# Order of the gate matrices, of the first value block and of the gate loads in a PEER layer

## The chip, the cores and the metric

The kernel runs on one NeuronCore of a Trainium2 chip. The metric is the device time of one execution in microseconds (us), lower is better; the time of a kernel is the median of its runs. Engines are named as the profile names them: PE (TensorE matmul), PEld (its weight loads), DVE (VectorE), ACT (ScalarE), POOL (GpSimd) and SP (SyncE, which only issues transfers here).

## The reference

One decoder layer for 512 tokens of width 1024. An attention sub-layer comes first (two groups of heads, not touched here). The second sub-layer is a mixture of 16384 one-neuron experts: each token looks up its 16 best experts for each of 8 heads with product keys, and sums their outputs.

```python
sc = jnp.einsum("bshpd,hpnd->bshpn", qp, sub_keys)      # two halves, 128 keys each
s1, i1 = lax.top_k(sc[..., 0, :], 16); s2, i2 = lax.top_k(sc[..., 1, :], 16)
cand = s1[..., :, None] + s2[..., None, :]
top_s, top_c = lax.top_k(cand.reshape(..., 256), 16)
expert = e1 * 128 + e2                                  # e1, e2 from i1, i2, top_c
gate = jax.nn.softmax(top_s, axis=-1)
a = einsum("bcd,bchkd->bchk", h, peer_u[expert])        # u_e . h
y = einsum("bchk,bchkd->bcd", gate * gelu(a), peer_v[expert])
x = x + gate2 * y
```

## The kernel before

The 512 tokens are four tiles of 128. Tile 0 (`SPARSE`) is done by gathers: 128 rows of `peer_u` and 128 of `peer_v` are fetched per token by indirect transfers from POOL, and DVE forms the dot products (`scr`, `sact`) and the weighted sum (`y`). Tiles 1 to 3 (`DENSE`, 384 tokens) are done densely against all 16384 experts, in 128 blocks of 128 experts, in two long loops.

The **unit blocks** (`ahead`, then `dense_u`): block b of U (`ut`, 512 KB) is loaded, split into a rounded part `uhi` (ACT) and a rest `ulo` (DVE), and multiplied with the hidden states in 24 matmuls of 384 columns (L935 to L937). ACT applies gelu (`ge`, L939), and for the first 120 blocks (`AHEAD`) the 192 KB result is stored to DRAM (`ged`).

The **value blocks** (`dense`): `ge` of block b comes back (L947), DVE multiplies it with the gates of that block (`gt`, L968), ACT and DVE split the product into `whl` (L971, L972), the block of V (`vt`, 512 KB) is split into `vhi` (ACT, L871) and `vlo` (DVE, L872), and 18 matmuls of 512 columns add it to six accumulators in PSUM (`acc`, L981). The last eight unit blocks are computed between value blocks.

The gates are dense matrices `G`, made from the lookup. For each dense tile `pick(i)` (12 steps, `choose` and `select`, on DVE and POOL) finds the 16 experts of each head, and `gates(i)` (48 steps in all, `gate_matrix`) builds 0/1 patterns on DVE, multiplies them on PE (16 short matmuls a step, L820), copies them out on ACT (`gst`, L822) and writes 1 MB to `G` every second step (L826). `work` is the list of these steps; the loop at the end of `build` takes some of them after each unit block.

`gt` holds the gates of eight value blocks (`GI`), 1536 KB, in two buffers. Buffers that the prediction uses: `whl` comes from pool `k3` with six buffers (L85), so its copy for block n waits until PE has finished block n - 6; `uhi`, `ulo`, `vhi` and `vlo` have two each (L870), so the copy to `vhi` for block m waits until PE has finished block m - 2; `ut` and `vt` have three.

The order of the instructions on each engine is not the order of the source. The pools and data set what may run, and a scheduler with its own estimate of times (`schedule_with_timeline_sim`) fixes one order for each engine when the kernel is built. Each engine then works strictly in that order.

Of the kernel before, what the change touches and what calls it, by code (L numbers as in the profile page):

```python
# [21 lines left out]
P = 128  # L22
# [9 lines left out]
NK = 128  # L32
# [6 lines left out]
DENSE = [1, 2, 3]  # L39
ND_T = len(DENSE) * P  # L40
GT = 16
NG = ND_T // GT
GI = 8
GSCALE = 4096.0
OT = 8
AHEAD = 120
# [32 lines left out]
class Layer:  # L79
# [814 lines left out]
    def ahead(self):  # L894

        self.ge = {}
        self.acc, self.vs = None, {}
        self.reopen()
        for b in range(AHEAD):
            self.dense_u(b)  # L900
            yield

    def dense(self):

        u = AHEAD
        for b in range(3):
            self.ge_in(b)
        for b in range(NK):
            self.ge_in(b + 3)
            self.v_in(b)  # L910
            if b < NK - 2:
                for t in range(len(DENSE)):
                    self.v_mm(b, t)
            elif b == NK - 1:
                for t in range(len(DENSE)):
                    self.v_mm(b - 1, t)
                    self.v_mm(b, t)
                    self.finish(DENSE[t], self.acc[t])
            for _ in range(min(NK - u, self.u_count(b, u))):
                self.dense_u(u)  # L920
                u += 1
            yield
# [4 lines left out]
    def dense_u(self, b):  # L927
        nc = self.nc
        pe = nc.tensor
        uh, ul = self.us.pop(b) if b in self.us else self.u_load(b)  # L930
        pa = self.bank() if b < AHEAD else self.bank2()
        A = pa[:, :ND_T]
        for k in range(KD):
            hh, hl = (z[k // 2][:, k % 2, :] for z in self.h2)
            pe.matmul(A, uh[:, k, :], hh, start=(k == 0), stop=False)  # L935
            pe.matmul(A, uh[:, k, :], hl, start=False, stop=False)  # L936
            pe.matmul(A, ul[:, k, :], hh, start=False, stop=(k == KD - 1))  # L937
        self.ge[b] = self.k2([P, ND_T], "ge")
        nc.scalar.activation(self.ge[b], A, AF.Gelu_apprx_tanh)  # L939
        if b < AHEAD:  # L940
            nc.sync.dma_start(self.ged[b], self.ge.pop(b))
# [4 lines left out]
            self.ge[b] = self.k2([P, ND_T], "ge")  # L946
            self.load(self.ge[b], self.ged[b])  # L947

    def gates_in(self, n):

        self.gtn = self.dn([P, NG, GI, GT], "gt")
        self.load(self.gtn, self.G[n])

    def v_in(self, b):

        nc, I = self.nc, self.I
        if b == 0:
            self.gates_in(0)
        if b % GI == 0:
            self.gt = self.gtn  # L960
        if b % GI == 4 and b + 4 < NK:
            self.gates_in(b // GI + 1)
        vt = self.dn([P, D], "vt", F32, 3)
        self.load(vt, I["peer_v"][b * P:(b + 1) * P, :])
        vh, vl = self.split(vt, "v", nc.vector)
        w = self.ge.pop(b)
        wg = w.rearrange("p (g t) -> p g t", t=GT)
        nc.vector.tensor_tensor(out=wg, in0=wg, in1=self.gt[:, :, b % GI, :], op=OP.mult)  # L968
        whl = self.k3([P, 2, ND_T], "whl", F32R)
        wh, wl = whl[:, 0], whl[:, 1]  # L970
        nc.scalar.copy(wh, w)  # L971
        nc.vector.tensor_tensor(out=wl, in0=w, in1=wh, op=OP.subtract)  # L972
        if self.acc is None:
            self.acc = [[self.bank(name="acc") for _ in range(2)] for _ in DENSE]
        self.vs[b] = (wh, vh), (wh, vl), (wl, vh)
# [24 lines left out]
    def build(self):  # L1000
# [17 lines left out]
        def seq(*gs):  # L1018
            for g in gs:
                yield from g  # L1020

        def weave(main, fill, n, skip=0, every=1, rest=True):
            for m, _ in enumerate(main):
                if m >= skip and (m - skip) % every == 0:
                    for _ in range(n):
                        next(fill, None)
            if rest:
                run(fill)
# [6 lines left out]
        def top(i, c):  # L1035
            self.best(i, T[i], c)
            yield
# [9 lines left out]
        def pick(i):  # L1047
            for hh in range(2):
                yield from self.choose(i, T[i], hh)

        def gates(i):
            yield from self.gate_matrix(i, *self.chosen[i])
# [32 lines left out]
        n = [self.hidden2(i, T[i]) for i in (3, 2, 1)]  # L1085
        run(pipe(o[:3] + [prep(self.w_pq, 0)] + o[3:5] + n[:1] + o[5:] + [prep(self.w_pq1, 3)] + n[1:] + [q1(3)], 2))
        for c in range(4):
            tops = [top(i, c - 1) for i in DENSE if 0 < c < 3] + ([top(0, 3)] if c == 1 else [])
            weave(self.queries(T, c), seq(*tops), 1)
        work = seq(pick(0), *(top(i, c) for c in (2, 3) for i in DENSE), *(pick(i) for i in DENSE),  # L1090
                   *(gates(i) for i in DENSE))
        sparse = self.sparse_steps(SPARSE)
        share = lambda n, of, steps: (n + 1) * steps // of - n * steps // of if 0 <= n < of else 0

        def gathered(steps):

            for _ in range(steps):
                with self.tc.issue_after(self.last_split.ins):
                    next(sparse, None)

        for n, _ in enumerate(self.ahead()):
            for _ in range(share(n, AHEAD - 8, 102)):
                next(work, None)
            gathered(share(n - 16, AHEAD - 16, 100))
        run(work)
# [50 lines left out]
```

## Time and profile before

| | before |
|---|---|
| median of 3 runs | 1693.03 us (1692.58 to 1693.55) |
| the profiled execution | 1691.5 us, span 1689.1 us |
| mean granted TensorE clock | 0.979 |
| PE busy | 1586.1 us, 94% of the span |
| unit blocks | about 492 to 1086 us |
| value blocks | about 1095 to 1674 us |

The span goes from the first to the last instruction; the execution's time is 2.4 us longer. Durations of matmuls overlap, so the step from one start to the next is what a matmul costs. A figure in brackets at the end of a timeline row is the idle time of that engine ahead of the instruction and what ended it.

### The profile page before, as it was taken

The numbers are of one execution on the slowest core, as the hardware profiler recorded it, in microseconds if no ns is written. First come the engines' busy times: TensorE is split into PE (matmuls) and PEld (weight loads), VectorE is DVE, ScalarE is ACT, GpSimd is POOL, SyncE is SP. The second block draws the span as 40 slices with busy tenths as digits, with TensorE's granted clock in tenths as the row PEclk, the third lists the DMA queues.
The fourth block names the chain that finished last, engine by engine and source line by source line (L and its number), as shares of the span: only waits on it lengthen the run. The fifth ranks groups of instructions, "written<-read, shape, count | busy, mean of one in ns | idle before, by whom it ended". The sixth has DMA issues, their size and how long they took to land.

```text
span 1689.1 us, 25030 instructions
## 1 busy us (share of the span) xinstructions
PE 1586.1 (94%) x8993; PEld 1390.9 (82%) x8993; DVE 1263.2 (75%) x2626; ACT 678.6 (40%) x1072; POOL 478.6 (28%) x514
## 2 busy tenths in 40 slices
PE   5999999998978999999999999799999999999996
PEld 2976498987977999999999999787777777877885
DVE  2624364585899679899989899488888888887863
ACT  3522364354224434334656656333333333333331
POOL 1303510001013355564213232123333333233311
PEclk8999999999989999999999999999999999999998
DMA  7354513368154688888999999999999999999852
GB/s 295 122 212 159 194 39 132 121 215 272 36 188 139 229 287 264 262 281 270 346 335 337 328 325 349 387 354 368 353 370 357 366 365 358 366 375 364 289 180 100
DMA packets 189391, 451.34 MB, mean 267 GB/s; under 512 B 16594, under 2 KB 102610, under 8 KB 185172
## 3 DMA queue, kind: packets, MB, share of 16 engines
q1 hardware_dynamic: 91732, 277.17, 46.1%
q0 software_dynamic: 38656, 139.48, 23.5%
q10 hardware_dynamic: 58880, 33.11, 6.5%
q8 instruction: 70, 1.15, 0.3%
q14 instruction: 53, 0.43, 0.1%
HBM read 393.07 MB, written 56.63 MB: 266 GB/s over the span
## 4 chain that ended last, share of the span: by engine, by line
PE 75%; DVE 11%; DMA 7%; ACT 2%; issue 2%; POOL 0%; POOLq 0%; SPq 0%; DVEq 0%; ACTq 0%
PE acc L981 27%; PE bank L937 8%; PE bank L936 8%; PE bank L935 8%; PE bank L386 4%; PE bank L173 4%; PE bank L387 4%; PE bank L385 4%; DVE ulo L872 3%; PE bank L820 3%; DMA vt<-in_peer_v 2%; PE bank L136 2%; PE bank L564 2%; PE bank L579 2%; DMA ge<-ged 1%
## 5 line engine op out<-in xcount | busy, mean ns | idle before, releaser
L981 PE MATMUL acc<-vhi,whl 128*128 128x512 f32 x1536 | 422.6, 395 | 25.7 <-ACT vhi L871 17.0
L981 PEld LDWEIGHTS acc<-vhi,whl 128*128 128x128 f32 x1536 | 289.0, 189 | 94.1 <-ACT vhi L871 21.7
L937 PE MATMUL bank<-hhi,ulo 128*128 128x384 f32 x1024 | 348.0, 340 | 17.2 <-DVE ulo L872 17.2
L935 PE MATMUL bank<-hhi,uhi 128*128 128x384 f32 x1024 | 346.3, 339 | 12.3 <-ACT uhi L871 12.2
L936 PE MATMUL bank<-hlo,uhi 128*128 128x384 f32 x1024 | 348.3, 340 | 0.0
L831 POOL DMA_INDIRECT gat<-in_peer_v,ids x128 | 158.4, 1238 | 348.2 <-DVE y L859 324.2
L871 ACT CAST uhi<-ut 128x1024 fp32r<-128x1024 f32 x128 | 134.5, 1051 | 304.5 <-PE bank L936 262.4
L981 PE MATMUL acc<-vlo,whl 128*128 128x512 f32 x768 | 241.0, 395 | 0.1
L831 POOL DMA_INDIRECT gat<-in_peer_u,ids x128 | 142.6, 1114 | 336.0 <-DVE sact L849 305.1
L872 DVE TENSOR_TENSOR ulo<-ut,uhi 128x1024 fp32r<-128x1024 f32 x128 | 178.5, 1395 | 63.6 <-ACT uhi L871 62.8
L937 PEld LDWEIGHTS bank<-hhi,ulo 128*128 128x128 f32 x1024 | 194.3, 190 | 23.0 <-DVE ulo L872 22.6
L935 PEld LDWEIGHTS bank<-hhi,uhi 128*128 128x128 f32 x1024 | 194.3, 190 | 14.2 <-ACT uhi L871 13.8
L936 PEld LDWEIGHTS bank<-hlo,uhi 128*128 128x128 f32 x1024 | 194.5, 190 | 0.5
L872 DVE TENSOR_TENSOR vlo<-vt,vhi 128x1024 fp32r<-128x1024 f32 x128 | 156.4, 1222 | 43.6 <-ACT vhi L871 42.7
L871 ACT CAST vhi<-vt 128x1024 fp32r<-128x1024 f32 x128 | 133.7, 1049 | 110.6 <-PE acc L981 85.4
L981 PEld LDWEIGHTS acc<-vlo,whl 128*128 128x128 f32 x768 | 145.1, 189 | 33.1 <-DVE vlo L872 1.2
L859 DVE SCALAR_TENSOR_TENSOR y<-gat,swgt,y 128x1024 f32<-128x1024 f32 x127 | 167.8, 1322 | 1.8 <-DMA gat<-in_peer_v,ids 1.7
L971 ACT CAST whl<-ge 128x384 fp32r<-128x384 f32 x128 | 65.4, 512 | 257.4 <-PE acc L981 240.1
L849 DVE CUSTOM_DVE_ANT_0 scr<-gat,h2r 128x1024 bf16<-128x1024 f32 x128 | 166.2, 1298 | 0.1
L972 DVE TENSOR_TENSOR whl<-ge,whl 128x384 fp32r<-128x384 f32 x128 | 70.8, 555 | 55.6 <-ACT whl L971 52.4
L822 ACT ACTIVATE gst<-bank 128x512 f32<-128x512 f32 x96 | 96.8, 1117 | 9.3 <-PE bank L820 4.7
L968 DVE TENSOR_TENSOR ge<-ge,gt 128x384 f32<-128x384 f32 x128 | 69.8, 552 | 17.7 <-DMA ge<-ged 15.6
(252 smaller groups left out, 2217.2 us busy)
## 6 DMA issues: line engine op xcount, KB each, us to landing
ut<-in_peer_uT SPq DMA_DIRECT2D x128, 512.0 KB
vt<-in_peer_v SPq DMA_DIRECT2D x128, 512.0 KB
G<-gst ACTq DMA_DIRECT2D x24, 1024.0 KB
gt<-G SPq DMA_DIRECT2D x16, 1536.0 KB
ged<-ge SPq DMA_DIRECT2D x120, 192.0 KB
ge<-ged SPq DMA_DIRECT2D x120, 192.0 KB
w<-in_w_ada SPq DMA_DIRECT2D x16, 1024.0 KB
w<-in_w_pq SPq DMA_DIRECT2D x32, 512.0 KB
```

Source lines behind the costliest of these rows:

```text
L822: nc.scalar.activation(st[:, :, q + t4:q + t4 + 4].rearrange("p i t -> p t i"), pb.rearrange("p (t i) -> p t i", t=4), AF.Copy, scale=1.0 ...
L831: self.nc.gpsimd.indirect_dma_start(out=t, out_offset=None, in_=self.I[table], in_offset=bass.IndirectOffsetOnAxis(ap=ids[:, k:k + 1], axi ...
L849: v.tensor_tensor_reduce(out=scr, in0=u, in1=self.rows, op0=OP.mult, op1=OP.add, scale=1.0, scalar=0.0, accum_out=a[:, k:k + 1])
L859: v.scalar_tensor_tensor(out=self.y, in0=t, scalar=w[:, k:k + 1], in1=self.y, op0=OP.mult, op1=OP.add)
L871: nc.scalar.copy(hi, src)
L872: self.last_split = eng.tensor_tensor(out=lo, in0=src, in1=hi, op=OP.subtract)
L935: pe.matmul(A, uh[:, k, :], hh, start=(k == 0), stop=False)
L936: pe.matmul(A, uh[:, k, :], hl, start=False, stop=False)
L937: pe.matmul(A, ul[:, k, :], hh, start=False, stop=(k == KD - 1))
L968: nc.vector.tensor_tensor(out=wg, in0=wg, in1=self.gt[:, :, b % GI, :], op=OP.mult)
L972: nc.vector.tensor_tensor(out=wl, in0=w, in1=wh, op=OP.subtract)
L981: self.nc.tensor.matmul(self.acc[t][half], w[:, ts], v[:, half * 512:(half + 1) * 512], start=(b == n == 0), stop=(b == NK - 1 and n == 2))
```

## The change

The list `work` is reordered: before, all three `pick` and then all three `gates`; now `gates(i)` follows `pick(i)` for each tile. The steps are spread over 108 unit blocks (106 of them) in place of 112 (102). The gates of value block group n are loaded in six parts of 256 KB, called for in six successive value blocks, in place of one load of 1536 KB. Those of the first group, the first three `ge` and the first block of V are called for among the last unit blocks; since this takes the accumulators' six PSUM banks, the last four unit blocks use the other two.

```diff
         for b in range(AHEAD):
             self.dense_u(b)
+            if AHEAD - 5 <= b < AHEAD - 2:
+                for q in range(2):
+                    self.gates_in(0, 2 * (b - AHEAD + 5) + q)
+                self.ge_in(b - AHEAD + 5)
             yield
+            if b == AHEAD - 2:
+                self.v_in(0)
...
     def dense(self):
         u = AHEAD
-        for b in range(3):
-            self.ge_in(b)
         for b in range(NK):
             self.ge_in(b + 3)
-            self.v_in(b)
+            if b:
+                self.v_in(b)
...
-        pa = self.bank() if b < AHEAD else self.bank2()
+        pa = self.bank() if b < AHEAD - 4 else self.bank2()
...
-    def gates_in(self, n):
+    def gates_in(self, n, q):
-        self.gtn = self.dn([P, NG, GI, GT], "gt")
-        self.load(self.gtn, self.G[n])
+        if q == 0:
+            self.gtn = self.dn([P, NG, GI, GT], "gt")
+        g = slice(q * NG // 6, (q + 1) * NG // 6)
+        self.load(self.gtn[:, g], self.G[n, :, g])
...
-        if b == 0:
-            self.gates_in(0)
         if b % GI == 0:
             self.gt = self.gtn
-        if b % GI == 4 and b + 4 < NK:
-            self.gates_in(b // GI + 1)
+        if b % GI < 6 and b // GI + 1 < NK // GI:
+            self.gates_in(b // GI + 1, b % GI)
...
-        work = seq(pick(0), *(top(i, c) for c in (2, 3) for i in DENSE), *(pick(i) for i in DENSE),
-                   *(gates(i) for i in DENSE))
+        work = seq(pick(0), *(top(i, c) for c in (2, 3) for i in DENSE),
+                   *(g for i in DENSE for g in (pick(i), gates(i))))
...
-            for _ in range(share(n, AHEAD - 8, 102)):
+            for _ in range(share(n, AHEAD - 12, 106)):
```

Since the scheduler sets the final order, three places of it are shown, before and after. A row is an instruction with its line, and xN says that it follows itself N times; the changed kernel's lines are five higher from `dense_u` on.

**First place: ACT, from the last unit blocks to the first value blocks.** Before, the copies to `uhi` of blocks 121 to 123 (the row with x3) stand ahead of the first `whl`:

```order
L871 CAST uhi<-ut 128x1024
L939 ACTIVATE ge<-bank 128x384
L871 CAST uhi<-ut 128x1024
L939 ACTIVATE ge<-bank 128x384 x2
L871 CAST uhi<-ut 128x1024 x3
L971 CAST whl<-ge 128x384 x5
L871 CAST vhi<-vt 128x1024
```

Now the first `whl` stands ahead of the copy for block 120 and of the last two gelus:

```order
L871 CAST uhi<-ut 128x1024 x2
L944 ACTIVATE ge<-bank_10965 128x384
L976 CAST whl<-ge 128x384
L871 CAST uhi<-ut 128x1024
L944 ACTIVATE ge<-bank_11006 128x384
L976 CAST whl<-ge 128x384 x2
L871 CAST uhi<-ut 128x1024
L944 ACTIVATE ge<-bank_11061 128x384
L871 CAST vhi<-vt 128x1024 x3
L976 CAST whl<-ge 128x384 x4
L871 CAST uhi<-ut 128x1024
```

The copies for blocks 122 and 123, which PE first needs after value block 109, have moved behind the first value blocks; on PE, value block 0 now starts inside unit block 119, and blocks 120 and 121 lie between value blocks 1 and 5.

**Second place: ACT, at value blocks 26 to 29.** The steady pattern is one `whl` (block n), then one `vhi` (block n - 4). Before, the three `whl` here are those of blocks 30 to 32, and the `vhi` around them those of blocks 25 and 26 and of 27 to 29:

```order
L971 CAST whl<-ge 128x384
L871 CAST vhi<-vt 128x1024 x2
L971 CAST whl<-ge 128x384 x3
L871 CAST vhi<-vt 128x1024 x3
L971 CAST whl<-ge 128x384 x2
L871 CAST vhi<-vt 128x1024
```

Now the `whl` of block 32 stands ahead of the `vhi` of block 27, and that of block 33 ahead of the `vhi` of block 28:

```order
L976 CAST whl<-ge 128x384
L871 CAST vhi<-vt 128x1024
L976 CAST whl<-ge 128x384 x2
L871 CAST vhi<-vt 128x1024
L976 CAST whl<-ge 128x384
L871 CAST vhi<-vt 128x1024 x2
L976 CAST whl<-ge 128x384
```

A `whl` five blocks ahead of the `vhi` that follows it stands in 11 places of the order before and in 14 of the changed one: ahead of the `vhi` of blocks 18, 27, 35, 42, 51, 59, 67, 74, 91, 99 and 106 before, and of 13, 19, 27, 28, 34, 42, 43, 51, 59, 66, 75, 91, 99 and 107 now.

**Third place: the SP queue, at the load of one group's gates.** Before:

```order
L281 DMA vt<-in_peer_v 128x1024
L281 DMA gt<-G 128x3072
L281 DMA ge<-ged 128x384
L281 DMA vt<-in_peer_v 128x1024
L281 DMA ge<-ged 128x384
L281 DMA vt<-in_peer_v 128x1024
```

The same load now; all six parts stand within two value blocks, as at the other groups:

```order
L281 DMA vt<-in_peer_v 128x1024
L281 DMA gt<-G 128x512
L281 DMA ge<-ged 128x384
L281 DMA gt<-G 128x512 x3
L281 DMA vt<-in_peer_v 128x1024
L281 DMA gt<-G 128x512 x2
L281 DMA ge<-ged 128x384
L281 DMA vt<-in_peer_v 128x1024
```

The parts for groups 0 and 1 stand far earlier, in six pairs among the loads of U. The first pair, here, comes after the store of unit block 43, while `gates(1)` is being written:

```order
L946 DMA ged<-ge 128x384
L281 DMA gt<-G 128x512
L281 DMA ut<-in_peer_uT 128x1024
L281 DMA gt<-G 128x512
L946 DMA ged<-ge 128x384
L281 DMA ut<-in_peer_uT 128x1024
```

Before, both groups were loaded one after the other just behind the load of unit block 122.

## Rows read from the trace of the kernel before

**Rows 1.** Page, part 1: busy time of each engine, share, instructions.

```profile
PE 1586.1 (94%) x8993; PEld 1390.9 (82%) x8993; DVE 1263.2 (75%) x2626; ACT 678.6 (40%) x1072; POOL 478.6 (28%) x514
```

**Rows 2.** Busy time by stretch of the span, with granted clock and transfers.

```profile
core 0: us, PE busy (x) PEld busy (x) DVE busy (x) ACT busy (x) POOL busy (x), PEclk, DMA share, GB/s
...
620.00:796.00 176.00, 165.88 (x934) 162.10 (x934) 166.13 (x233) 62.15 (x88) 103.66 (x99) 0.98 0.84 265
796.00:1064.00 268.00, 268.00 (x2029) 259.89 (x2028) 239.00 (x324) 168.47 (x205) 65.22 (x53) 1.00 1.00 338
...
1095.00:1101.00 6.00, 5.86 (x14) 4.60 (x15) 5.20 (x11) 2.10 (x5) 0.00 (x0) 0.50 1.02 366
...
1112.00:1172.00 60.00, 60.00 (x261) 48.66 (x261) 51.85 (x74) 20.06 (x29) 22.81 (x19) 1.00 1.00 388
1172.00:1557.00 385.00, 368.45 (x1589) 297.61 (x1587) 320.20 (x435) 130.99 (x181) 127.43 (x111) 1.00 0.98 365
```

**Rows 3.** Timeline of ACT between unit and value blocks.

```profile
1081.77 1.05 ACT L871 CAST uhi<-ut 128x1024 fp32r<-128x1024 f32 x1 [0.71 <-DMA ut<-in_peer_uT]
1093.49 1.04 ACT L871 CAST uhi<-ut 128x1024 fp32r<-128x1024 f32 x1 [10.67 <-DMA ut<-in_peer_uT]
1094.58 0.51 ACT L971 CAST whl<-ge 128x384 fp32r<-128x384 f32 x1
```

**Rows 4.** Timeline of SP's transfers there.

```profile
1071.95 1.94 SPq L281 DMA_DIRECT2D gt<-G  x2
...
1077.80 0.33 SPq L281 DMA_DIRECT2D ut<-in_peer_uT  x1
```

**Rows 5.** Timeline of PE there.

```profile
1081.11 0.44 PE L935 MATMUL bank<-hhi,uhi 128*128 128x384 f32 x1 [1.04 <-ACT uhi L871]
...
1082.37 0.44 PE L937 MATMUL bank<-hhi,ulo 128*128 128x384 f32 x1 [0.65 <-DVE ulo L872]
...
1095.14 1.22 PE L981 MATMUL acc<-vhi,whl 128*128 128x512 f32 x2 [8.66 <-ACT whl L971]
```

**Rows 6.** Waits from 1110 to 1558 us: total, times, longest.

```profile
PE acc L981 <- ACT vhi L871: 17.0, 11, 1.5
...
ACT vhi L871 <- DMA vt<-in_peer_v: 8.2, 7, 1.9
```

**Rows 7.** Timeline of ACT at value block 18.

```profile
1168.88 0.51 ACT L971 CAST whl<-ge 128x384 fp32r<-128x384 f32 x1 [2.62 <-PE acc L981]
1173.07 0.51 ACT L971 CAST whl<-ge 128x384 fp32r<-128x384 f32 x1 [3.68 <-PE acc L981]
1173.49 1.99 ACT L871 CAST vhi<-vt 128x1024 fp32r<-128x1024 f32 x2
```

**Rows 8.** Timeline of PE at value block 18.

```profile
1172.41 0.63 PE L981 MATMUL acc<-vhi,whl 128*128 128x512 f32 x2
1174.58 1.67 PE L981 MATMUL acc<-vhi,whl 128*128 128x512 f32 x6 [1.55 <-ACT vhi L871]
```

**Rows 9.** Timeline of PE at value block 82.

```profile
1451.99 1.97 PE L981 MATMUL acc<-vhi,whl 128*128 128x512 f32 x8
1454.04 0.74 PE L981 MATMUL acc<-vlo,whl 128*128 128x512 f32 x2
```

**Rows 10.** Timeline of ACT at value block 82.

```profile
1451.01 1.05 ACT L871 CAST vhi<-vt 128x1024 fp32r<-128x1024 f32 x1 [1.93 <-DMA vt<-in_peer_v]
```

**Rows 11.** Waits from 620 to 800 us, PE's largest.

```profile
PE bank L937 <- DVE ulo L872: 10.1, 10, 2.4
```

**Rows 12.** Timeline of ACT while gates are written.

```profile
1001.51 0.37 ACTq L826 DMA_DIRECT2D G<-gst  x1
...
1015.19 2.00 ACT L822 ACTIVATE gst<-bank 128x512 f32<-128x512 f32 x2 [2.33 <-DMA G<-gst]
1016.97 1.07 ACT L871 CAST uhi<-ut 128x1024 fp32r<-128x1024 f32 x1
...
1021.87 1.05 ACT L871 CAST uhi<-ut 128x1024 fp32r<-128x1024 f32 x1 [1.52 <-DVE vhi L812]
```

## The prediction

> **What bounds the kernel now.** The page's first part says PE: busy for 94% of the span [rows 1]. An average over stages does not price a change, so the second view is the busy time by stretch [rows 2], and there the reader should compare PE's busy time with the length of each stretch. From 796 to 1064 us, where the gates are built and written, PE is busy for all 268 us: that stretch is as long as PE's work, and moving its steps elsewhere moves time without saving any. From 620 to 796, where the experts of tiles 1 to 3 are picked, PE idles for 10 of 176 us. In the value stretch from 1172 to 1557 it idles for 16.6 of 385, while the transfers show a share of 0.98. So the questions are what PE waits for at three places: while picking, between the last unit block and the first value block, and in the value stretch.
>
> The third view is the timeline between the two loops. PE is held for 1.04, 0.65 and 8.66 us, the last one by the first `whl` on ACT [rows 5]. ACT had nothing to compute: it stood 10.67 us at the copy of a unit block that waits for its transfer, with the first `whl` right behind [rows 3]. By the order of ACT that copy is of block 123, which PE wants only after value block 109. Its load was issued at 1077.80, behind two loads of 1536 KB issued from 1071.95 [rows 4], and the copy began 15.7 us later. Then PE ran at a granted clock of 0.50 from 1095 to 1101 us: 14 matmuls in 6.00 us, where 261 later took 60.00, or 0.230 each [rows 2].
>
> The fourth view is the waits of the value stretch: PE waited for `vhi` 11 times, 17.0 us together, at most 1.5 each [rows 6]. Waits so alike come from an order, not from late transfers. At block 18, ACT runs a `whl` at 1168.88, stands 3.68 us for PE, runs another `whl`, and only then the `vhi` for which PE is idle [rows 7]. With six `whl` buffers and two of `vhi`, a `whl` five blocks ahead of the next `vhi` cannot run before PE has finished the block just before the one that needs that `vhi`; PE then waits for one `whl` and one `vhi`. The order of before has 11 such places, the trace 11 waits.
>
> **The change, part by part.** *Between the loops.* The copies of blocks 122 and 123 move behind the first value blocks, and the gates of groups 0 and 1 are loaded far earlier, so nothing is left that holds the first `whl`. Removed: 1.04 + 0.65 + 8.66 = 10.35 us [rows 5], and the half clock behind it, 6.00 - 14 x 0.230 = 2.8 us [rows 2]; 13.2 in sum. PE's new order there (value block 0 inside unit block 119) needs the first `vhi`, `ge` and gates by then; all are loaded while unit blocks still run. What may be late next is a `vhi` of blocks 2 to 4, which waits for PE to finish the block two before; units 120 and 121 lie between as cover. Bounds 0 and two waits of the kind in the value stretch, 3.4; I take 0.5, near the lower end for that cover.
>
> *Value stretch.* One such place costs PE more than the idle that the profile shows: two matmuls start from 1172.41, a third was due 0.46 later at 1172.87 and began at 1174.58 [rows 8], 1.71 us late. The changed order has 14 places, 3 more: +5.1. Bounds: 0, if at the two doubled groups (27 and 28, 42 and 43) the second wait finds PE already supplied, and 8.5, if a late load adds one more wait at each of these two groups. I take 5.1, because the count met the trace 11 for 11.
>
> *Loads in six parts.* The source spreads them over six value blocks; the order does not, it puts all six within two. The bytes ahead of the second `vt` behind a group are those of before. The place without the ACT order shows what a late `vt` alone costs: at block 82 `vhi` waited 1.93 us for its transfer [rows 10], and PE, eight matmuls on from 1451.99 and so due at 1453.83, went on at 1454.04 [rows 9], 0.2 late. So 0 here. If the transfers were the bound, the upper end: 14 groups of 1.57 MB, 22.0 MB, at 338 in place of 365 GB/s, both from stretches with a share of about 1 [rows 2], 65.1 - 60.3 = 4.8.
>
> The Trainium skill speaks against this edit: "DMA: Bandwidth & Descriptors", section "Measured (HBM→SBUF, 128 partitions, SWDGE, issued from GpSimd)", asks for batches of 1 MiB or more, and the fit under "Anatomy of one DMA — SWDGE (gpsimd) path" gives a fixed 2.0 us plus bytes over 436 GB/s. By that fit, an estimate, six parts take 15.6 us one after the other and one load 5.6; without overlap that would be 140 us over 14 groups. No row here shows a part of 256 KB; the sum goes by the bounds above.
>
> *Gate parts among the unit blocks.* New waits on SP: the first pair of parts needs four writes of `G` of which the last was issued just before, and the loads of U stand behind. One write, issued at 1001.51, was still waited for at 1015.19 [rows 12], so SP stands for at most 13.7 us. The held load has three buffers, so about two unit blocks in hand, 4.9 us each by the copies at 1016.97 and 1021.87 [rows 12]; at most 3.9 us remain, at three places, 0 to 11.7. I take 0.5: 13.7 is a write that was waited for, and the store ahead of the pair takes some of it.
>
> *Picking.* The 36 steps stand between gate steps now, and a little denser (106 in 108 blocks, before 102 in 112). They cost PE 10.1 us of waiting for `ulo`, in 10 waits [rows 11], and a clock of 0.98 over 176 us, 3.5 more [rows 2]: 13.6 in all. Denser steps load DVE more; the gate blocks between let it catch up, though only slowly (239 of 268 us busy [rows 2]). I take 0, with half of 13.6 to either side.
>
> **Sum.** 1691.5 for the profiled execution, - 13.2 + 0.5 + 5.1 + 0.5 + 0 = 1684.4. That execution was 1.5 below the median of 1693.0, so the median comes to 1685.9.
>
> **Rivals.**
>
> *The unit stretch takes the gain back.* Denser picking and the holds on SP both reach their upper halves, some +4 to +10: 1690 to 1696, no measurable change. For it: DVE is busy 166 of 176 us while picking [rows 2], and a hold by a write is certain, only its cover is not. Against: PE had no idle at all in the 268 us of gate blocks, at the same share of transfers. 0.20.
>
> *Transfers pace the value stretch.* Then PE's savings count for nothing; what helps is that two groups, 3.1 MB, now move earlier (3.1 MB at 365 GB/s, -8.6), and the parts cost 4.8: 1693.0 - 8.6 + 4.8 = 1689.2, at the edge of no change. For it: a share of 0.98. Against: 388 GB/s from 1112 to 1172 against 365 later [rows 2], so transfers can go faster. The Trainium skill's rule on batches, cited above, points this way. 0.10.
>
> *Slower: the values behind each group come later.* Six parts and a `ge` now stand between two loads of `vt`, and if both blocks behind a group lose a further 1.71, 14 groups cost 23.9: 1709.8. It decides from 0.75 us a group on, 10.5 in all, since that leads to 1696.4. For it: 7 waits for `vt`, 8.2 us [rows 6], so these loads are only just in time. Against: block 82, 1.93 us late for 0.2. 0.12.
>
> *Faster still.* Picking in three separate runs lets DVE catch up and halves its 13.6, or the doubled places cost nothing: 1676 to 1682. 0.08.
>
> **How the numbers follow.** My forecast, 1682 to 1689, has 0.50. What a measurement of this kernel can tell from no change is about 0.2%, 3.4 us, so faster means below 1689.6 and slower above 1696.4. Faster: 0.50 + 0.08 and a little under half of the transfers' case, 0.62. Slower: 0.12 and the edge of the first rival, 0.13. Same: the rest, 0.25. A range from 1678 to 1694 holds the forecast, most of the first rival, the transfers' case and most of the last one, about 0.82.
>
> **What would show it.** Between the loops: no idle of PE above 2 us and a clock of 1.00; a copy to `uhi` waiting for a transfer ahead of the first `whl` would refute that step. In the value stretch: PE waits for `vhi` 14 times, some 22 us; 11 or fewer, or waits above 2 us, would refute the count. While picking: waits for `ulo` of about 10 us, now in three groups. On SP: three waits for writes of `G`, and no copy to `uhi` that waits for its transfer just after them. The prediction is wrong above all if PE idles among the unit blocks of gates, where it now never does.

## The result

Measured side by side, the changed kernel takes 1681.99 us (median of 4 runs, 1680.49 to 1686.27) and the kernel before 1693.29 (4 runs): ratio 0.9938, 95% interval 0.9921 to 0.9955, 11.3 us less. Timed once more on another occasion (e9 below) it took 1683.23 against 1693.27, ratio 0.9947, 0.9929 to 0.9965. It is faster, by some 0.6%.

The profile that stands beside this is that of the slowest of the four runs, 1686.27 us. The busy time by stretch comes first (columns as in [rows 2]); the kernel before, in the stretch ahead of the unit blocks, which the change doesn't touch:

```profile
0.00:490.00 490.00, 454.44 (x2840) 377.56 (x2840) 273.54 (x1070) 196.24 (x436) 82.59 (x158) 0.97 0.46 159
```

And the changed kernel, there and in the stretches of [rows 2]:

```profile
0.00:490.00 490.00, 457.56 (x2831) 380.81 (x2832) 270.06 (x1051) 195.18 (x434) 81.80 (x156) 0.96 0.45 156
620.00:796.00 176.00, 168.88 (x1119) 163.75 (x1117) 166.91 (x255) 88.94 (x114) 84.85 (x80) 0.99 0.93 307
796.00:1030.00 234.00, 232.30 (x1665) 226.29 (x1666) 215.51 (x282) 131.24 (x163) 82.28 (x64) 1.00 0.97 327
1030.00:1064.00 34.00, 32.08 (x184) 31.40 (x183) 18.06 (x20) 11.84 (x17) 7.26 (x8) 1.00 0.99 356
1064.00:1112.00 48.00, 48.00 (x243) 43.43 (x242) 37.02 (x50) 17.92 (x26) 12.54 (x12) 1.00 0.99 357
1172.00:1557.00 385.00, 365.36 (x1576) 294.79 (x1574) 317.39 (x431) 129.20 (x179) 123.19 (x111) 1.00 0.98 360
```

In the first 490 us this execution had a lower clock, 0.96 against 0.97, and its first unit matmul started 3.8 us later (496.5 against 492.6). In e9's profile, of a run of 1680.99 us, it started at 492.1. From the first unit matmul to the last value matmul the kernel before took 1181.3 us, this execution 1172.8 and e9's 1171.7: 8.5 and 9.6 less. That is the part in which the change acts, and by which the terms are judged below. PE is as busy as in [rows 1], by the page's first part:

```profile
PE 1586.5 (94%) x8993; PEld 1392.5 (83%) x8993; DVE 1261.8 (75%) x2626; ACT 679.3 (40%) x1072; POOL 483.4 (29%) x514
```

Between the loops (1064 to 1112) PE is busy for all 48 us at full clock; that is the stretch with the holds of [rows 5]. In the value stretch it idles for 19.6 us, 3.1 more than in [rows 2]. From 796 to 1064, where it had no idle, it now has 3.6. The waits of the value stretch (1110 to 1558 us; total, times, longest), which answer to [rows 6]:

```profile
PE acc L986 <- ACT vhi L871: 22.7, 15, 1.5
...
ACT vhi L871 <- DMA vt<-in_peer_v: 6.5, 7, 1.2
```

The forecast was 14 waits and some 22 us. By the starts of the matmuls, 14 lie at the 14 blocks named in front, each 1.71 or 1.72 us late; the fifteenth, 1.26 us at 1382.7, is a second late start behind one of them, and e9's profile hasn't got it (21.7 us in 14 waits). The timeline of SP near the last unit blocks shows what the forecast had least of:

```profile
1037.18 0.33 SPq L281 DMA_DIRECT2D ut<-in_peer_uT  x1
1047.86 0.88 SPq L281 DMA_DIRECT2D gt<-G  x2
```

SP issued nothing for 10.3 us, because the pair of gate parts waited for a write of `G`. By the waits of SP from 620 to 1076 us this happens 8 times:

```profile
SPq L281 <- DMA G<-gst: 39.9, 8, 10.2
```

In the kernel before it was 9.9 us in 3 waits. ACT shows what came of it, in the copies of unit blocks ahead of the first `whl` (the last row here):

```profile
1055.97 1.04 ACT L871 CAST uhi<-ut 128x1024 fp32r<-128x1024 f32 x1 [3.81 <-DMA ut<-in_peer_uT]
...
1060.12 1.05 ACT L871 CAST uhi<-ut 128x1024 fp32r<-128x1024 f32 x1 [2.71 <-DMA ut<-in_peer_uT]
...
1071.93 0.50 ACT L976 CAST whl<-ge 128x384 fp32r<-128x384 f32 x1
```

And PE, for which the first of these copies was late by 1.28 us of idle and its `ulo` by 0.64:

```profile
1057.06 0.44 PE L940 MATMUL bank<-hhi,uhi 128*128 128x384 f32 x1 [1.28 <-ACT uhi L871]
...
1058.32 0.44 PE L942 MATMUL bank<-hhi,ulo 128*128 128x384 f32 x1 [0.64 <-DVE ulo L872]
```

This hold belongs to the one execution. In e9's profile, SP again:

```profile
986.56 0.33 SPq L281 DMA_DIRECT2D ut<-in_peer_uT  x1
995.35 1.58 SPq L281 DMA_DIRECT2D gt<-G  x2
...
1025.77 0.33 SPq L281 DMA_DIRECT2D g<-g2d  x1
...
1027.49 1.17 SPq L281 DMA_DIRECT2D ut<-in_peer_uT  x1
...
1034.40 0.33 SPq L281 DMA_DIRECT2D ut<-in_peer_uT  x1
1036.17 2.83 SPq L281 DMA_DIRECT2D gt<-G  x2
```

The last pair waits for no write there. The pair at 995.35 waited 8.4 us and made no matmul late. But the load of U issued at 1027.49, behind the load of `g2` (a row for the last sums, which waited 2.7 us for a write of `G` and stands in the kernel before too), came late, and PE with it, by 2.7 us at 1040. On ACT in e9:

```profile
1038.76 1.05 ACT L871 CAST uhi<-ut 128x1024 fp32r<-128x1024 f32 x1 [7.65 <-DMA ut<-in_peer_uT]
```

### The profile page after: what moved, and what is told of

Its sections match the earlier page's. It is cut to its first block, busy times and chain, and to the rows that moved or that the text cites. A ratio compares the mean times of both kernels' runs of the same rounds, so it can differ in the third digit from the quotient of the medians.

```text
span 1684.5 us, 25155 instructions
## 1 busy us (share of the span) xinstructions
PE 1586.5 (94%) x8993; PEld 1392.5 (83%) x8993; DVE 1261.8 (75%) x2626; ACT 679.3 (40%) x1072; POOL 483.4 (29%) x514
## 4 chain that ended last, share of the span: by engine, by line
PE 77%; DVE 10%; DMA 5%; ACT 3%; issue 2%; POOL 0%; SPq 0%; POOLq 0%; ACTq 0%; DVEq 0%
PE acc L986 30%; PE bank L942 7%; PE bank L941 7%; PE bank L940 7%; PE bank L386 4%; PE bank L387 4%; PE bank L173 4%; PE bank L385 4%; DVE ulo L872 3%; PE bank L820 2%; PE bank L136 2%; DMA G<-gst 2%; PE bank L564 2%; PE bank L579 2%; DMA ut<-in_peer_uT 1%
## 5 line engine op out<-in xcount | busy, mean ns | idle before, releaser
L942 PE MATMUL bank<-hhi,ulo 128*128 128x384 f32 x1024 | 347.1, 339 | 15.4 <-DVE ulo L872 15.3
L940 PE MATMUL bank<-hhi,uhi 128*128 128x384 f32 x1024 | 345.5, 338 | 12.5 <-ACT uhi L871 12.4
L872 DVE TENSOR_TENSOR ulo<-ut,uhi 128x1024 fp32r<-128x1024 f32 x128 | 170.7, 1334 | 58.1 <-ACT uhi L871 57.7
L849 DVE CUSTOM_DVE_ANT_0 scr<-gat,h2r 128x1024 bf16<-128x1024 f32 x128 | 170.8, 1334 | 0.0
L822 ACT ACTIVATE gst<-bank 128x512 f32<-128x512 f32 x96 | 96.9, 1120 | 6.3 <-DMA G<-gst 6.3
L772 POOL TENSOR_TENSOR prod<-hit,cid 128x800 f32<-128x800 f16 x32 | 70.6, 2207 | 20.6 <-DVE hit L769 18.4
```

Of the source, the lines that this page charges most:

```text
L772: g.tensor_tensor(out=prod, in0=hit, in1=cid[:, r][:, None, :, None].to_broadcast(shape), op=OP.mult)
L822: nc.scalar.activation(st[:, :, q + t4:q + t4 + 4].rearrange("p i t -> p t i"), pb.rearrange("p (t i) -> p t i", t=4), AF.Copy, scale=1.0 ...
L849: v.tensor_tensor_reduce(out=scr, in0=u, in1=self.rows, op0=OP.mult, op1=OP.add, scale=1.0, scalar=0.0, accum_out=a[:, k:k + 1])
L872: self.last_split = eng.tensor_tensor(out=lo, in0=src, in1=hi, op=OP.subtract)
```

## The experiments

Theory: the gain is what PE lost between the loops, and the ACT order gives 1.71 us back at each place of a `whl` five blocks ahead; loads in six parts cost nothing. Rivals: late loads of `vt`, not the order of ACT, hold the value stretch; and one part of the change alone does it all. "Late" below is the step from one matmul's start to the next, less its usual step.

### The order of ACT (e1, e2)

Both queue the `whl` of block n on ACT behind the `vhi` of block n - 4, e1 in the changed kernel, e2 in the one before, which takes away all such places:

```diff
-        nc.scalar.copy(wh, w)
+        with self.tc.issue_after(self.casts[b - 4].ins) if b > 3 else nullcontext():
+            nc.scalar.copy(wh, w)
```

> The changed kernel with one constraint more: on ACT the copy to whl of value block n is queued behind the copy to vhi of block n-4; nothing else is edited. Theory (each whl five blocks ahead of the next vhi costs PE 1.71 us): the waits of PE for vhi fall from 15 (22.7 us of idle) to a few of some tenths, and the time falls by 20 to 25 us, from 1682 to 1657-1662. Rival (transfers pace the value stretch): the idle turns up as waits for vt, and the gain is under 6 us.

> The kernel before with the same constraint on ACT. Theory: 11 waits of 1.71 us go, 16 to 19 us faster than before, 1674-1677; the hold of 8.7 us between the loops stays, so it stays 12 to 17 us slower than the run of the changed kernel with the constraint. Rival (transfers pace the value stretch): under 5 us faster than before.

e2: 1678.24 us, ratio 0.9931 (0.9907 to 0.9956) to the kernel before (1691.44 there, as for e1 to e4). That is 13.2 us less by the medians, under the 16 to 19 of the theory. The profile is of a run of 1674.10 us (the four go up to 1683.69), and in it the time from first unit to last value matmul fell by 19.2 us; 11 x 1.71 is 18.8. The hold between the loops stays, as it should. Its busy time in the value stretch:

```profile
1172.00:1557.00 385.00, 384.79 (x1671) 313.70 (x1670) 333.52 (x455) 136.01 (x189) 121.42 (x117) 1.00 1.00 380
```

PE has 0.2 us of idle in place of 16.6. So in this execution the price of a place is confirmed, and with it that the transfers did not pace this stretch. Why the median fell short is open.

e1: 1671.57 us (1660.85 to 1678.32, a wide spread), ratio 0.9881 (0.9839 to 0.9924). From first unit to last value matmul it gained 15.4 us on the changed kernel; the theory had 20 to 25. Its waits from 1110 to 1558 us:

```profile
ACT vhi L871 <- DMA vt<-in_peer_v: 94.9, 30, 7.3
...
PE acc L988 <- ACT vhi L871: 4.8, 6, 1.6
...
PE acc L988 <- DVE vlo L872: 1.3, 3, 0.7
```

The waits for the order are gone, and `vhi` now waits 30 times for `vt` (7 times in the changed kernel). PE is late by some 7.6 us there, behind the clusters of gate parts. SP at one of them, in e1:

```profile
1250.54 1.56 SPq L281 DMA_DIRECT2D gt<-G  x3
1252.20 0.56 SPq L281 DMA_DIRECT2D vt<-in_peer_v  x1
1252.85 0.58 SPq L281 DMA_DIRECT2D ge<-ged  x1
1253.49 2.44 SPq L281 DMA_DIRECT2D gt<-G  x3
1257.61 0.33 SPq L281 DMA_DIRECT2D vt<-in_peer_v  x1
```

ACT after it:

```profile
1261.42 1.05 ACT L871 CAST vhi<-vt 128x1024 fp32r<-128x1024 f32 x1 [3.41 <-DMA vt<-in_peer_v]
...
1267.96 1.05 ACT L871 CAST vhi<-vt 128x1024 fp32r<-128x1024 f32 x1 [5.08 <-DMA vt<-in_peer_v]
```

So both are true in their place: the order of ACT sets the changed kernel's pace, and hides loads that are late and would show next.

A wait of `vhi` is not by itself a cost, though. e2, with one load of 1536 KB a group, has such waits too (1110 to 1558 us), and PE is late by only 0.4 us there:

```profile
ACT vhi L871 <- DMA vt<-in_peer_v: 64.2, 21, 4.7
```

So under the same constraint on ACT, the kernel with six parts in clusters lost some 7 us that the one with one load a group did not. e1 and e2 differ in the rest of the change too; the changed kernel with one load and the constraint was not run.

### Where the parts stand (e3, e4, e10)

e3 is e1 with the parts of groups 0 and 1 queued on SP behind the store of the unit block ahead of which they are called for, so none stands early. e4 is e3 with each further part queued behind the load of V called for just before it: now six parts do stand over six blocks; the third piece below is e4's alone. e10 is e4 without the edit on ACT (4 places by its order).

```diff
-            nc.sync.dma_start(self.ged[b], self.ge.pop(b))
+            self.last_sp = nc.sync.dma_start(self.ged[b], self.ge.pop(b))
...
-        self.load(self.gtn[:, g], self.G[n, :, g])
+        with self.tc.issue_after(self.last_sp.ins):
+            self.load(self.gtn[:, g], self.G[n, :, g])
...
-        self.load(vt, I["peer_v"][b * P:(b + 1) * P, :])
+        t = nc.sync.dma_start(vt, I["peer_v"][b * P:(b + 1) * P, :])
+        if b > 4:
+            self.last_sp = t
```

> The changed kernel with the ACT constraint, and the gate parts of groups 0 and 1 queued on SP behind the unit stores that stand ahead of them in the source, so that none is issued before its writes of G have landed. Theory (SP's 39.9 us of waiting for writes of G cost PE 2.2 us through late loads of U): PE's idle of 1.4 and 0.8 us at 1055 us goes, 1 to 4 us faster than with the ACT constraint alone. Rival (the early loads were what freed the stretch between the loops): value block 0 waits for its gates, 3 to 10 us slower than with the ACT constraint alone.

> As the run with late gate parts, and each further gate part queued on SP behind the load of one vt, so that the six parts really spread over six value blocks. Theory (the place of the parts matters little, since the bytes are the same): within 3 us of the run with late parts. Rival (six parts within two value blocks make both vt behind them late): waits of ACT's vhi for vt fall and it is 5 us or more faster.

> The changed kernel with each part of a group's gates queued on SP behind the load of V that is called for just before it, so that six parts stand over six value blocks, and with the parts of groups 0 and 1 behind the unit stores called for before them; the order of whl and vhi on ACT is left to the scheduler, and has 4 places in place of 14. Theory (late vt behind a cluster of parts and the ACT order are two costs, and spreading removes the one and most of the other): no wait of vhi for vt, PE waits 4 times 1.71 = 6.8 us, so some 7 us above the version with both edits (1659.1): 1664 to 1668, 15 us or more below the changed kernel. Rival (only the ACT order counts, where the loads stand is worth nothing): 10 places of 1.71 fewer, 17 us, and the late loads still show, 1665 at best and up to 1672, with PE waits behind vt of several us.

e3: 1669.97 us, ratio 0.9876 (0.9861 to 0.9891): 1.6 us below e1, and not told apart from it. Of the 2.4 us at the late load of U in e1, 0.8 are left, but a `whl` is late by 1.82 us instead. Nor are all holds gone: SP still waits 15.1 us for writes of `G`, in 2 waits, at the loads of `g2` and `x` (a tile for the last sums), which use the buffers of `gst`. The late `vt` stayed (waits from 1110 to 1558 us):

```profile
ACT vhi L871 <- DMA vt<-in_peer_v: 101.2, 31, 6.9
```

e4: 1659.14 us, ratio 0.9814 (0.98 to 0.9829), 10.8 below e3, where the theory had under 3: my step "loads in six parts cost nothing" holds only while another wait covers them. SP in e4, one part a block:

```profile
1242.28 0.33 SPq L970 DMA_DIRECT2D vt<-in_peer_v  x1
1242.67 0.42 SPq L281 DMA_DIRECT2D gt<-G  x1
...
1246.47 0.33 SPq L970 DMA_DIRECT2D vt<-in_peer_v  x1
1246.85 0.42 SPq L281 DMA_DIRECT2D gt<-G  x1
```

Its wait of `vhi` for `vt` from 1110 to 1558 us:

```profile
ACT vhi L871 <- DMA vt<-in_peer_v: 6.0, 2, 3.1
```

And its busy time in the value stretch:

```profile
1172.00:1557.00 385.00, 385.00 (x1680) 315.49 (x1679) 335.46 (x455) 136.12 (x190) 140.59 (x118) 1.00 1.01 380
```

101.2 us in 31 waits became 6.0 in 2, and PE's late starts in the value stretch 0.5 us in place of 9.0, with the same bytes. PE has no idle at a transfer share of 1.01 and 380 GB/s; the changed kernel moved 360 with 0.98. A share near 1 was no bound.

e10: 1674.69 us, ratio 0.9906 (0.9874 to 0.9937), above the theory's 1664 to 1668. The four places are there, each 1.71 us late, but so are late loads (waits from 1110 to 1558 us):

```profile
ACT vhi L871 <- DMA vt<-in_peer_v: 32.0, 18, 4.5
...
PE acc L989 <- ACT vhi L871: 6.2, 4, 1.5
PE acc L989 <- DVE vlo L872: 5.5, 7, 2.1
```

Spreading alone does not bring the loads in time; with the order of ACT tied down it does. Why they are late in e10 is not settled.

### The parts of the change alone (e5 to e8)

The kernel before was 1693.39 us beside these four (14 runs). The edits are pieces of the diff in front. e5 is before with the part loads alone; e6 is before with the first value block, gates and `ge` among the last unit blocks, and with 106 steps over 108 blocks; e8 is before with the interleaved list and the same 106 over 108 (the list has 102 steps, so it is done some four blocks before the 108 are over); e7 is the changed kernel with one load of 1536 KB a group:

```diff
-        if q == 0:
+        if q == 5:
             self.gtn = self.dn([P, NG, GI, GT], "gt")
-        g = slice(q * NG // 6, (q + 1) * NG // 6)
-        self.load(self.gtn[:, g], self.G[n, :, g])
+            self.load(self.gtn, self.G[n])
```

> Before with the six part loads alone: lookup, gates, first value block and shares as before. By the order of the instructions the parts of groups 0 and 1 stand far earlier among the loads of U, the copies to uhi of the last unit blocks still stand ahead of the first whl, and the value loop has 13 places of a whl five blocks ahead in place of 11. Theory (PE's hold between the loops came from the 3.1 MB of gates in front of the last loads of U): the copy that stood 10.67 us now waits under 3 us, so the hold of 8.66 us and the half clock behind it are gone, -9 to -13, and two more places cost +3.4: 5 to 10 us faster than before. Rival (the order of copies ahead of whl makes the hold): it stays, and with the places the kernel is 3 us slower than before, or the same.

> Before with the first value block, the first group's gates and the first three ge called for among the last unit blocks, and the lookup spread over 106 of 108 blocks; the lookup is not interleaved with the gates and a group's gates come in one load of 1536 KB. By the order: the first whl stands ahead of the copies of units 121 to 123, 10 places in the value loop in place of 11. Theory: the whole term between the loops, -13.2, is won by this part alone, and -1.7 for the place: 12 to 17 us faster than before, 1675 to 1681, a little below the changed kernel, since the denser spread costs nothing. Rival (the gain of the changed kernel comes from the lookup in three groups): under 6 us.

> The changed kernel with one load of 1536 KB a group in place of six parts. By the order, gates of groups 0 and 1 are loaded behind the last writes of G, as before, and the value loop has 10 places in place of 14. Theory: no early parts, so the late load of U at about 1055 (1.44 + 0.80 us of PE) is gone, and four or five places of 1.71 fewer: 8 to 10 us faster than the changed kernel, 1672 to 1676. Rival 1 (early parts are what empties the stretch between the loops): the hold of 8.66 comes back, and it is no faster than the changed kernel. Rival 2 (the places cost nothing of their own, transfers pace the value loop): the same as the changed kernel within 3 us.

> Before with the lookup and the gates of each tile interleaved and spread over 106 of 108 blocks, nothing else. By the order: the two loads of gates now stand behind the load of unit 114 in place of unit 122, two copies to uhi still ahead of the first whl, 10 places in place of 11. Theory: picking is 3.4 us cheaper (waits for ulo and half clock there 10 in place of 13.6), the place gives 1.7, and the hold between the loops falls by more than half, since the loads of U have several blocks to catch up: 8 to 14 us faster than before, with PE's longest idle between the loops under 4 us. Rival (picking is not what changed, it differs from run to run): 1.7 for the place and what the hold gives, and waits for ulo of 10 us or more.

| | time | ratio to before | PE late between the loops | places of 1.71 |
|---|---|---|---|---|
| e5 parts only | 1693.52 | 0.9995 (0.9981 to 1.0009) | 9.05 | 13 |
| e6 first V early | 1685.94 | 0.9954 (0.9937 to 0.9970) | 7.33 + 0.67 | 10 |
| e8 interleaved | 1684.58 | 0.9953 (0.9938 to 0.9967) | 9.78 + 0.60 | 10 |
| e7 changed, one load | 1685.39 | 0.9948 (0.9931 to 0.9965) | 7.46 + 2.09 + 1.40 | 10 |

The places are right four times out of four: 13, 10, 10 and 10 late starts of 1.71 or 1.72 us, at the blocks that the order names. The theory on the hold is wrong in e5, e6 and e8, and in e7 the rival with the hold was right: each leaves 7 to 10 us and a stretch at half clock. e5 has no 3.1 MB in front of the last loads of U, yet SP stands there:

```profile
1075.80 0.33 SPq L941 DMA_DIRECT2D ged<-ge  x1
1085.21 0.80 SPq L281 DMA_DIRECT2D gt<-G  x2
1086.11 0.38 SPq L281 DMA_DIRECT2D ut<-in_peer_uT  x1
```

This last pair needs the last write of `G` (issued at 1064.24), and the copy ahead of the first `whl` stands as before, on ACT in e5:

```profile
1092.47 1.04 ACT L871 CAST uhi<-ut 128x1024 fp32r<-128x1024 f32 x1 [8.77 <-DMA ut<-in_peer_uT]
1095.28 0.98 ACT L974 CAST whl<-ge 128x384 fp32r<-128x384 f32 x2 [1.76 <-DVE ge L971]
```

and PE waits for that `whl`, as in [rows 5]:

```profile
1095.84 1.22 PE L984 MATMUL acc<-vhi,whl 128*128 128x512 f32 x2 [8.89 <-ACT whl L974]
```

In e7 SP stands 7.0 us once, at the load of `g2` issued at 1025.88; behind it the two loads of 1536 KB are in front of the loads of U:

```profile
1036.82 0.33 SPq L281 DMA_DIRECT2D ut<-in_peer_uT  x1
1038.28 1.89 SPq L281 DMA_DIRECT2D gt<-G  x2
...
1042.59 0.33 SPq L281 DMA_DIRECT2D ut<-in_peer_uT  x1
```

and PE waits for a `uhi` that it wants now (waits of PE in e7, 600 to 1100 us):

```profile
PE bank L940 <- ACT uhi L871: 9.2, 2, 7.3
```

e8 has both, a hold of 10.7 us and the two loads behind it. So neither the parts alone (e5: the copy ahead of `whl` and SP's hold are left) nor the first value block among the unit blocks without them (e6, e7: the 3.1 MB are left) empties this stretch; the changed kernel has both. It also has the new list, and no run has both without it: the last write of `G` goes out at 1061.4 before, 1064.2 in e5, 1044.3 in e6 and 1024.7 to 1029.2 with the new list, so what that adds is not told apart. That a hold of SP alone costs as much is not shown: holds of 8 to 11 us in the changed kernel, e3, e9 and e10 cost PE 0 to 2.2.

The times of e6, e7 and e8 are nevertheless near the changed kernel's, by other routes. Against the kernel before, by lateness as in the table of the next section, e6 gives 1.9 us while picking, 4.4 from 1030 to 1112 and 2.3 in the value stretch; e8 3.8, 1.4 and 2.7; e7 3.8, 0.8 and 1.8. What the changed kernel wins over e7 from 1030 to 1112, 11.1 us, it mostly pays back in the value stretch, 7.7, of which four more places make 6.9: e7's interval and the changed kernel's overlap. So the rival that one part alone does it all holds for most of the time gained, with the interleaved list (e8) or the early first value block (e6), each with the denser spread, but not for the place where it is gained.

### Once more, and a version without these waits (e9, e11)

e9 is the changed kernel. e11 is e4 with the loads of `g2` and `x` for the last sums queued behind the loads of V; in e4 the load of `g2` stood among the last loads of U, its buffer not free before a write of `G` was done. The wait of SP in e4, 620 to 1100 us:

```profile
SPq L281 <- DMA G<-gst: 6.9, 1, 6.9
```

```diff
-        self.load(self.mods["g2"], self.g2d.to_broadcast([P, D]))
+        with self.tc.issue_after(self.last_sp.ins):
+            self.load(self.mods["g2"], self.g2d.to_broadcast([P, D]))
...
-        self.load(x, self.xd[i])
+        with self.tc.issue_after(self.last_sp.ins):
+            self.load(x, self.xd[i])
```

> The changed kernel once more, beside the next two on one chip and for a second profile. Both theories: 8 to 12 us faster than before. By the order, the same 14 places of 1.71 us in the value loop, no hold between the loops. The one wait of 1.26 us that stood outside the 14 places (a second vt behind a doubled group, at 1382.7) is either there again (it belongs to the order) or gone (it was that execution's).

> The version with both edits (1659.1), and the loads of g2 and x for the last sums queued behind the last loads of V, so that they no longer stand on SP among the loads of U. Theory (SP stood 6.9 us for a write of G with the load of g2, and the loads of U behind it came late): the idle of PE of 1.73 + 0.80 us near 1040 is gone, 2 to 4 us faster, 1655 to 1658. Rival (the loads of U are late for another reason): the idle stays, 1659.

e9 is told above. e11: 1653.63 us (1651.89 to 1654.98), ratio 0.9766 (0.9750 to 0.9783), 2.3% below the kernel before, some 30 us below the changed one and 5.5 below e4, where the theory had 2 to 4. All waits of PE from 600 to 1558 us in e11:

```profile
PE bank L942 <- DVE ulo L872: 7.8, 7, 2.3
```

Only the lookup's waits are left. The late `uhi` near 1040 is gone, and so are starts late by 2.8 us near 1095 to 1120 that e4 still had, which the theory had not; why these went is open.

## Why the prediction was right, and where it was not

The time fell in the range and 4 us below the forecast, at the lower edge of the 1682 to 1689 that had most of the weight. The table goes by lateness: the step from each matmul's start to the next, less the median step of its shape, summed over a stretch. Half clock counts in it, and the rows add up to the time between the first unit and the last value matmul. The two columns on the right are the two profiles of the changed kernel, less the kernel before.

| term (stretch) | forecast | first profile | e9 |
|---|---|---|---|
| hold and half clock between the loops (1064 to 1112) | -13.2 + 0.5 | -13.9 | -13.8 |
| value stretch (from 1112) | +5.1 | +5.9 | +5.1 |
| late loads of U behind holds of SP (1030 to 1064) | +0.5 | +1.9 | +2.4 |
| picking (600 to 1030) | 0 | -2.8 | -3.2 |
| ahead of 600 | | +0.3 | -0.1 |
| sum | -7.1 | -8.5 | -9.6 |

So the sum was met in part by luck: picking gave 3 us that were not forecast, and the late loads of U took back half of them.

- **Between the loops.** The whole term came, with no idle from 1064 to 1112 us and full clock. The residual of 0.5 for a late `vhi` did not. But the test that I set was wrong: copies to `uhi` do wait for a transfer ahead of the first `whl` (3.81 and 2.71 us), and PE had cover at the `whl`. And the reason was incomplete: I named the order of ACT and the early gates together and did not say whether one would do; e5 and e6, of which I then expected that each would, show that neither did by itself.
- **Value stretch.** The count of places from the order, at 1.71 us, was the best step: 14 forecast, 14 found, and 13, 10, 10, 10 in other kernels; e2 removes them and, in its profile, gains what they cost. The extra 1.26 belongs to one execution.
- **Loads in six parts.** 0 was right for this kernel and wrong as a property of the loads. I argued from block 82, where one late `vt` cost 0.2 us; once the order no longer hides them, clusters cost some 10 us (e3 against e4). The rival "values behind each group come later" had the right mechanism, and only the cover kept it from showing. Nor do parts gain anything over one load a group in the value stretch: PE is late by 0.4 us in e2 and by 0.5 in e4. The estimate from the Trainium skill ("DMA: Bandwidth & Descriptors", section "Anatomy of one DMA — SWDGE (gpsimd) path"), 140 us for parts one after the other, is not met: e4, with 96 parts spread, has no idle of PE in the value stretch from 1172 us on. The Trainium skill's rule there, batches of 1 MiB or more, which it draws from loads issued from GpSimd, goes with clusters (e1 against e2) and not with parts that stand one a block (e4). In e3 against e4, with the size the same, the place in the queue decides.
- **Gate parts among the unit blocks.** The mis-sized term. I counted three waits of SP and no late `uhi`; there were 8 waits, 39.9 us, and one cost 2.2 us of PE in the first profile. The sentence that failed there is that about two blocks in hand cover the hold: SP stood 10.2 us up to 1047.86, the next load of U left it at 1049.78, its copy began at 1055.97, and PE had run dry at 1055.5. In e9 the cover held for the gate parts (8.4 us for nothing), and the loss came behind the load of `g2`, which the forecast did not look at. e11 moves `g2` and `x` away and has no late load of U. Both losses lay within the bounds of 0 to 11.7. The sign that I called the gravest, PE idle among the unit blocks of gates, did come (3.6 us from 796 to 1064), half of it from these loads and half from the picking of tile 3, which now stands there.
- **Picking.** Forecast 0, found -2.8 and -3.2. Part of it is one piece of 3.4 us at half clock in place of two, 1.7 less; but such pieces do not always follow the edits (e2, with the old list and spread, has one, e1, with the new ones, two), so that part may be chance. By late starts alone, each above 0.3 us, picking costs 11.8 us before, 12.5 and 11.8 in e2 and e5, which have the old list and spread; 11.0 in e6, which has the old list and the denser spread; and 9.3 to 10.1 in e7, e8, e9 and the changed kernel, which have both new. So the interleaved list seems to give more than the spread, against my step that DVE catches up only slowly between the groups; neither was tried by itself.
- **Rivals.** "Transfers pace the value stretch" falls with e2, e4 and e11. "The unit stretch takes the gain back" happened with the sign of SP's part, and picking went the other way. "Faster still" (0.08) had the sign of picking right, and the time lies at its upper edge, 1682; the doubled places cost their full price.

## What to carry to other kernels

Where a scheduler fixes the order of each engine, count in that order the places where an instruction that needs an old buffer back stands ahead of one that PE needs next: here each cost 1.71 us, the count met the trace in seven kernels, and one constraint on ACT took them all away, at some risk that late loads show next. A load that waits for a write holds every load behind it on its queue, so look for what stands behind it before asking whether it is itself needed soon. A wait that covers another one makes the second look free: price an edit again when the first wait is gone.

## What the runs showed that was not expected

A transfer share of 0.98 looked like a bound and was not: the value stretch moved 365 GB/s with PE idle 4% of the time, and 380 at a share of 1.01 when PE had no idle. Nor do the waits of `vhi` for late loads tell by their length what PE loses: 64.2 us of them cost 0.4 in e2, and 94.9 cost 7.6 in e1. And one kernel's two profiles differ in what holds it: the changed kernel lost its 2 us at the late loads of U behind the gate parts in one and behind the load of `g2` in the other.
